# Moving one filler tile between the two scans of a Mamba-2 layer, and halving two fillers

## The chip, the core and the metric

The kernel runs on one core of a Trainium2 chip. The metric is device time in microseconds (us) of one execution; the median of three runs stands for a kernel. Five engines work side by side, each through its own instructions in order: PE (TensorE, matmuls; PEld is its weight load), DVE (VectorE), ACT (ScalarE), POOL (GpSimd) and SP (SyncE, which issues all DMAs here). They wait for each other on semaphores.

## The reference

One encoder layer with 1024 tokens of width 1024: a half feed-forward step, an input projection, then attention and a state-space part (SSD) side by side, an output projection `concat(a, s) @ W_out`, a second feed-forward step and a gated embedding. The change lies in the state-space part and in the half of the output projection that belongs to attention. What the state-space part computes, per direction, in 8 chunks of 128 tokens (8 heads of width 64, two groups, state of 128):

```python
seg = a_cum[..., :, None] - a_cum[..., None, :]
Lmat = jnp.exp(jnp.where(tril, seg, -jnp.inf))
cb = jnp.einsum('bclgn,bcsgn->bcgls', c_c, b_c)
y_diag = jnp.einsum('bcgls,bgrcls,bcsgrp->bclgrp', cb, Lmat, xd)
decay_states = jnp.exp(a_cum[..., -1:] - a_cum)
states = jnp.einsum('bcsgn,bgrcs,bcsgrp->bcgrpn', b_c, decay_states, xd)
# scan over chunks: h -> h * d + st, prev is h before the chunk
y_off = jnp.einsum('bclgn,bcgrpn,bgrcl->bclgrp', c_c, prev, jnp.exp(a_cum))
...
y = y_f + y_b + d_skip * xh
y = y * silu(z);  y = rms over each group of 256;  ssd_out = y * ssd_norm
mix = concat(att_out, ssd_out) @ w_out
```

The backward direction is the same scan over the flipped sequence.

## The kernel before

All PE instructions stand in the order in which the program is written. The other engines' instructions, and SP's DMAs, are put in an order by a scheduler that knows the dependencies; it may move them past each other.

The state-space part follows the attention and has two passes over the chunks.

**The right pass** (`ssd_right`) runs from chunk 7 down to chunk 0 in a software pipeline of ten turns `i = 0 .. 9`. Turn i does `front` of chunk 7-i, `mid`, `offdiag` and `next_state` of chunk 8-i, and `back` of chunk 9-i:

- `front` (PE L1348, then ACT L1350; PE L1354, then ACT L1356): the decay exponents of both directions in two PSUM tiles, their exponentials `Ef` and `Eb`, and the product `cb` of B and C. It also loads the chunk two further on.
- `mid` (DVE L1361, L1362, L1365): `y` is the skip term; `W = (Eb + Ef) * cb` for both directions at once.
- `offdiag` (PE L1270, then DVE L1272 and L1273): C times the state that came from the chunks before, scaled, added to `y`.
- `next_state` (ACT L1264 scales x into `xs`, PE L1281, ACT L1264 scales the old state by the chunk's decay, DVE L1287 adds; for a first state DVE copies, L1284).
- `back` (PE L1371, DVE L1372): W times x, added to `y`, and a DMA stores `y` to `yd` in DRAM (L1373). There are three `y` buffers, so `mid` of a chunk waits for the store of the chunk three before it.

**The left pass** (`ssd_left`) runs from chunk 0 up to 7 with the forward direction's `offdiag` and `next_state`, loads `y` back from `yd`, adds, multiplies by the gate z (L1439), normalises (L1443 to L1449) and transposes `y` on PE for the output projection (`turn`, L1417, three chunks behind).

**Fillers** stand between the steps of both passes: PE work that depends on nothing near. A filler is the attention half of the output projection for one row tile of 128 tokens: it loads the residual row from `y0` in DRAM into an accumulator, does 24 matmuls (L122) in two column halves of 12, and adds each half's PSUM tile into the accumulator on DVE (`out_proj`, L1464; L1466 in the changed kernel). Row tiles 0 to 2 run in the right pass (`spilled`), and their accumulators `accr` (two buffers) go out to `y1` in DRAM; row tiles 3 to 7 run in the left pass (`resident`) and their accumulators `acc` stay in SBUF, in memory that the right pass's accumulators use before. All matmul results of both passes, but the exponents, share four PSUM buffers `sm`.

Before the change row tiles 0 and 1 stand at the end of turns 0 and 1, row tile 2 stands in turn 8 ahead of that turn's `offdiag` (chunk 0), and the left pass begins with the whole of row tile 3, then its first `next_state`, then `offdiag` of chunk 1.

Of the kernel before, what the change touches and what calls it, by code (L numbers as in the profile page):

```python
# [9 lines left out]
F32 = mybir.dt.float32  # L10
# [3 lines left out]
ALU = mybir.AluOpType  # L14
# [4 lines left out]
P = 128  # L19
S = 1024  # L20
D = 1024
NT = S // P
# [14 lines left out]
class Layer:  # L37
# [1288 lines left out]
    def ssd_right(self, c, loaded, fillers):  # L1326

        nc, tc = self.nc, self.tc
        V = nc.vector
# [29 lines left out]
        def mid(ch, xb, bc, E, cb):  # L1359
            y = two.tile([P, 512], F32, name="y", bufs=3)  # L1360
            V.tensor_tensor(out=self.heads(y), in0=self.heads(xb[:, :512]), in1=self.per_head(dsk), op=ALU.mult)  # L1361
            V.tensor_tensor(out=E[1], in0=E[1], in1=E[0], op=ALU.add)  # L1362
            W = E[1]
            for g in range(2):
                V.tensor_tensor(out=W[:, 4 * g:4 * g + 4], in0=W[:, 4 * g:4 * g + 4], in1=cb[:, g].unsqueeze(1).broadcast_to([P, 4, P]), op=ALU.mult)  # L1365
            return W, y

        def back(ch, xb, bc, W, y):
# [7 lines left out]
        F, B = {}, {}  # L1376
        for i in range(NT + 2):
            ch = NT - 1 - i
            if ch >= 0:
                F[ch] = front(ch)  # L1380
            if 0 <= ch + 1 < NT:
                c1 = ch + 1
                xb, bc, E, cb = F.pop(c1)
                B[c1] = (c1, xb, bc) + mid(c1, xb, bc, E, cb)
                if c1 == 0:
                    fillers.pop(i)()
                if st is not None:
                    self.offdiag(two, st, 1, c1, bc, B[c1][4])
                if c1 > 0:
                    st = self.next_state(two, st, 1, c1, xb)  # L1390
            if ch + 2 < NT:
                back(*B.pop(ch + 2))
            if i in fillers:
                fillers[i]()

    def ssd_left(self, c, loaded, late, mixT, fillers):

        nc, tc = self.nc, self.tc
        V = nc.vector
# [26 lines left out]
        for ch in range(NT):  # L1426
            xb, bc = loaded[ch]
            zs, y = rest.pop(ch)
            if st is not None:
                self.offdiag(two, st, 0, ch, bc, y)  # L1430
            if ch == 0:
                fillers.pop(0)()
            if ch < NT - 1:
                st = self.next_state(two, st, 0, ch, xb)
            if len(waiting) > 2:
                turn(*waiting.pop(0))
            if 0 < ch < NT - 1:
                load(ch + 1)
            V.tensor_tensor(out=y, in0=y, in1=zs, op=ALU.mult)  # L1439
            ss = self.small.tile([P, 2], F32, name="yss")  # L1440
            for g in range(2):
                sq = late.tile([P, 256], F32, name="ysq")
                nc.scalar.activation(out=sq, in_=y[:, g * 256:(g + 1) * 256], func=AF.Square, accum_out=ss[:, g:g + 1])  # L1443
            V.tensor_scalar(out=ss, in0=ss, scalar1=1.0 / 256, scalar2=RMS_EPS, op0=ALU.mult, op1=ALU.add)
            r = self.small.tile([P, 2], F32, name="yr")
            self.rsqrt(r, ss, 2)
            for g in range(2):
                o = slice(g * 256, (g + 1) * 256)
                V.scalar_tensor_tensor(out=y[:, o], in0=y[:, o], scalar=r[:, g:g + 1], in1=snorm[:, o], op0=ALU.mult, op1=ALU.mult)  # L1449
            waiting.append((ch, y))  # L1450
            if ch:
                fillers.pop(0)()
# [78 lines left out]
    def run(self):  # L1531
        nc, tc, I = self.nc, self.tc, self.I
# [6 lines left out]
        y0 = self.dram.tile([NT, P, D], F32, name="y0")  # L1539
# [29 lines left out]
        with ExitStack() as c:  # L1569
# [12 lines left out]
            mixT = [[self.unit(h, 0)] for h in range(2)]  # L1582
# [6 lines left out]
        wm = [[], []]  # L1589
# [13 lines left out]
                blocks = blocks0  # L1603
            wm[half].extend(zip(blocks[:4], blocks[4:]))

        def attention_half(t, a):
            nc.sync.dma_start(out=a, in_=y0[t])
            self.out_proj(t, 0, wm[0], mixT, a)

        sctx = ExitStack()  # L1610
        late = sctx.enter_context(tc.tile_pool(name="slate", bufs=2))
        self.ld = sctx.enter_context(tc.tile_pool(name="sload", bufs=4))
        loaded = {}
        with ExitStack() as c:
            def spilled(t):
                a = self.accr.tile([P, D], F32, name="accr")
                attention_half(t, a)
                nc.sync.dma_start(out=y1[t], in_=a)

            weights(0)  # L1620
            for h in range(2):
                mixT[h].append(self.unit(h, 1))
            self.ssd_right(c, loaded, {i: lambda t=t: spilled(t) for t, i in enumerate((0, 1, 8))})
        rctx.close()
        actx = ExitStack()
        ap = actx.enter_context(tc.tile_pool(name="acc1", bufs=8, side="right"))
# [3 lines left out]
            nc.sync.dma_start(out=dst, in_=I[name])  # L1630
        acc = {}

        def resident(t):
            acc[t] = ap.tile([P, D], F32, name="acc1")
            attention_half(t, acc[t])
            if t == NT - 1:
                weights(1)

# [23 lines left out]
        def mixed(t):  # L1662
            r = Row(t)
            for step in (lambda: r.half(0), lambda: r.half(1), r.root, r.factors, r.shift):
                step()
# [13 lines left out]
                nc.scalar.activation(out=to[k // 4][:, k % 4], in_=ps[k // 4][:, k % 4], func=AF.Identity, scale=gT[:, k:k + 1], bias=bT[:, k:k + 1])  # L1679

        with ExitStack() as c:
            fillers = [lambda t=t: resident(t) for t in range(3, NT)] + [lambda t=t: mixed(t) for t in range(3)]
            self.ssd_left(c, loaded, late, mixT, fillers + [lambda: mixed(3), lambda: (flip(0), mixed(4))])
        sctx.close()
        dctx.close()
# [289 lines left out]
```

## Time and profile before

| | |
|---|---|
| time, median of 3 runs | 1952.08 us (1951.97 to 1953.29) |
| the profiled execution's own time | 1952.0 us |
| its span, first to last instruction | 1950.2 us |
| PE busy | 1927.4 us, 99% of the span |
| DVE busy | 1526.2 us, 78% |
| ACT busy | 880.9 us, 45% |
| the right and the left pass on PE | from 1064.6 to about 1189 us of the span |

The profile's times count from the first instruction. A row of the timeline has start, length, engine, source line, operation, tiles and how many equal instructions it merges; in brackets stands how long the engine sat idle before it and what released it. A matmul's length reaches to the modelled arrival of its result, while the next one starts earlier, so how long a group keeps PE is read from the start of one group to the start of the next. An fp32 matmul shows as two.

### The profile page before, as it was taken

How to read it: one execution, taken by the hardware profiler on the slowest of the kernel's cores; microseconds unless marked ns; L12 is line 12 of the kernel's file. 1: busy time of each engine (PE TensorE's matmuls, PEld its weight loads, DVE VectorE, ACT ScalarE, POOL GpSimd, SP SyncE). 2: the span in 40 equal slices, each digit the busy share in tenths (PEclk: the TensorE clock that was granted, in tenths of full speed). 3: DMA queues.
4: the chain of work that ended last, by engine and by line, in shares of the span. 5: the costliest groups of instructions: out<-in, count | busy, mean ns of one | idle time of the engine just before them, and what ended most of it. 6: DMA issues, size and time to landing. Idle time of an engine off the chain costs nothing.

```text
span 1950.2 us, 25647 instructions
## 1 busy us (share of the span) xinstructions
PE 1927.4 (99%) x9132; PEld 1607.7 (82%) x9132; DVE 1526.2 (78%) x2364; ACT 880.9 (45%) x1509; POOL 416.0 (21%) x310
## 2 busy tenths in 40 slices
PE   8999999999999999999999999999999999999998
PEld 7888888888888889888888788888888888888886
DVE  7977777867678658758998878997686777877698
ACT  6433333325444224537887775733333333443311
POOL 0144545430001032001221001013544440001011
PEclk9999999999999999999999999999999999999999
DMA  8434554549866111231002383244545439986122
GB/s 301 138 125 154 191 179 151 194 164 373 294 221 208 61 38 59 82 120 61 6 1 88 132 290 114 92 161 163 189 155 185 163 129 354 334 262 225 33 76 98
DMA packets 147713, 310.34 MB, mean 159 GB/s; under 512 B 18128, under 2 KB 30800, under 8 KB 147584
## 3 DMA queue, kind: packets, MB, share of 16 engines
q1 hardware_dynamic: 147584, 308.69, 45.2%
q8 instruction: 72, 1.18, 0.3%
q14 instruction: 57, 0.47, 0.1%
HBM read 217.21 MB, written 91.42 MB: 158 GB/s over the span
## 4 chain that ended last, share of the span: by engine, by line
PE 95%; DVE 3%; ACT 1%; issue 0%; DMA 0%; POOL 0%; DVEq 0%; SPq 0%; ACTq 0%
PE sm L122 59%; PE big L516 12%; PE sm L516 9%; PE big L122 3%; PE big L1159 3%; PE sm L1181 2%; PE sm L1196 1%; PE sm L1197 1%; PE sm L1270 1%; PE sm L1371 1%; DVE nm L1166 1%; DVE conv L977 1%; PE sm L1281 0%; PE big L1677 0%; PE big L224 0%
## 5 line engine op out<-in xcount | busy, mean ns | idle before, releaser
L122 PE MATMUL sm<-xh,blk 128*128 128x512 f32 x1424 | 439.9, 389 | 0.0
L122 PEld LDWEIGHTS sm<-xh,blk 128*128 128x128 f32 x1424 | 267.3, 188 | 55.4
L122 PE MATMUL sm<-xl,blk 128*128 128x512 f32 x736 | 283.8, 389 | 0.0
L122 PE MATMUL sm<-blk,xl 128*128 128x512 f32 (+2 forms) x784 | 238.1, 371 | 0.2 <-ACT xn_t L1010 0.2
L122 PE MATMUL sm<-blk,xh 128*128 128x512 f32 (+2 forms) x584 | 202.7, 378 | 0.4 <-DVE accr L1464 0.4
L108 ACT CAST blk<-raw 128x512 fp32r<-128x512 f32 (+1 forms) x168 | 101.1, 610 | 214.6 <-PE sm L122 132.0
L87 DVE TENSOR_TENSOR blk<-s,blk 128x512 fp32r<-128x512 f32 x176 | 150.1, 857 | 38.3 <-ACT blk L108 36.5
L87 DVE TENSOR_TENSOR blk<-raw,blk 128x512 fp32r<-128x512 f32 (+1 forms) x168 | 144.9, 866 | 38.4 <-ACT blk L108 37.6
L108 ACT CAST blk<-s 128x512 fp32r<-128x512 f32 x172 | 105.8, 622 | 145.1 <-PE sm L122 114.7
L122 PEld LDWEIGHTS sm<-blk,xl 128*128 128x128 f32 x784 | 142.8, 188 | 24.2 <-ACT xn_t L1010 0.5
L122 PEld LDWEIGHTS sm<-xl,blk 128*128 128x128 f32 x736 | 138.1, 188 | 28.7
L178 POOL TENSOR_TENSOR ln_k<-ln_k,mhalf 128x1 f32<-128x1 f32 x32 | 36.6, 1149 | 583.3 <-DVE ln_k L177 578.3
L516 PE MATMUL big<-xh 128*128 128x512 f32 x576 | 138.8, 390 | 0.0
L267 POOL TENSOR_TENSOR s<-raw 128x512 f32<-128x512 f32 x34 | 55.1, 1620 | 384.4 <-DVE blk L87 378.2
L87 DVE TENSOR_TENSOR xh<-blk,xh 128x1024 fp32r<-128x1024 f32 x78 | 96.4, 1236 | 46.2 <-ACT xh L462 37.1
L462 ACT CAST xl<-blk 128x1024 fp32r<-128x1024 f32 x76 | 80.2, 1055 | 115.1 <-PE sm L516 41.4
L462 ACT CAST xh<-blk 128x1024 fp32r<-128x1024 f32 x78 | 82.3, 1055 | 106.0 <-PE big L516 49.2
L122 PEld LDWEIGHTS sm<-blk,xh 128*128 128x128 f32 x584 | 109.8, 188 | 19.9 <-DVE accr L1464 0.8
L516 PEld LDWEIGHTS big<-xh 128*128 128x128 f32 x576 | 107.8, 188 | 22.2
L87 DVE TENSOR_TENSOR xl<-blk,xl 128x1024 fp32r<-128x1024 f32 x76 | 92.6, 1219 | 41.9 <-ACT xl L462 37.2
L516 PE MATMUL big<-xl 128*128 128x512 f32 x480 | 115.7, 390 | 0.0
L122 PE MATMUL sm<-xET2h,blk 128*128 128x512 f32 x352 | 108.4, 389 | 0.0
(343 smaller groups left out, 4014.0 us busy)
## 6 DMA issues: line engine op xcount, KB each, us to landing
raw<-in_wi_dram SPq DMA_DIRECT2D x81, 512.0 KB
blk<-hS SPq DMA_DIRECT2D x154, 256.0 KB
hS<-h SPq DMA_DIRECT2D x88, 256.0 KB
wr<-in_wo_dram SPq DMA_DIRECT2D x44, 512.0 KB
blk<-wT SPq DMA_DIRECT2D x88, 256.0 KB
hS<-sg SPq DMA_DIRECT2D x66, 256.0 KB
wT<-wr SPq DMA_DIRECT2D x66, 256.0 KB
blk<-in_wo_dram SPq DMA_DIRECT2D x66, 256.0 KB
```

The lines of the kernel that those rows point to most:

```text
L87: (eng or self.nc.vector).tensor_tensor(out=out, in0=full, in1=hi.bitcast(F32), op=ALU.subtract)
L108: self.nc.scalar.copy(out=b[:, 0, :n], in_=src)
L122: self.nc.tensor.matmul(ps, lhsT=a, rhs=b, start=(i == 0), stop=(i == n - 1))
L178: nc.gpsimd.tensor_tensor(out=r, in0=v, in1=self.mhalf[:, :1], op=ALU.pow)
L267: lambda: G.tensor_tensor(out=s1, in0=a21, in1=a22, op=ALU.add),
L462: A.copy(out=b[:, :, 0], in_=r)
L516: nc.tensor.matmul(ps[q], lhsT=b[:, 0, x, cut], rhs=b[:, 1, y], start=j == i == 0, stop=j == NP - 1 and i == 2)
L977: nc.vector.scalar_tensor_tensor(out=a[:, o], in0=ps[:, o.start + d - c:o.stop + d - c], scalar=cw[:, j, tap:tap + 1], in1=a[:, o], op0=AL ...
L1159: nc.tensor.matmul(ps[:, n * 512:(n + 1) * 512], lhsT=Q[:, h, q0:q0 + P], rhs=K[:, h // 4, j, n * 512:(n + 1) * 512], start=j == 0, stop=j ...
L1166: nc.vector.tensor_reduce(out=nm, in_=ps, axis=AX.X, op=ALU.max, negate=True)
L1181: nc.tensor.transpose(out=pt[:, k], in_=pr[:, kk * P:(kk + 1) * P], identity=self.ident)
L1196: nc.tensor.matmul(po, lhsT=vw, rhs=pth[k // 4][:, k % 4], start=k == 0, stop=False)
```

## The change

Four edits:

- Row tile 2 leaves turn 8. Its first column half now stands at the end of turn 4 (behind `back` of chunk 5) and its second at the end of turn 5 (behind `back` of chunk 4). The accumulator's load goes with the first half, its store to `y1` with the second.
- In turn 8, where row tile 2 stood, `back` of chunk 1 now stands ahead of `offdiag` of chunk 0.
- In the left pass row tile 3 runs in halves too, and the first `next_state` stands between them.
- In `mid` the product with `cb` is one DVE instruction of 1024 elements per partition instead of two of 512 (one for each group).

```diff
             W = E[1]
-            for g in range(2):
-                V.tensor_tensor(out=W[:, 4 * g:4 * g + 4], in0=W[:, 4 * g:4 * g + 4], in1=cb[:, g].unsqueeze(1).broadcast_to([P, 4, P]), op=ALU.mult)
+            Wg = W.rearrange("p (g h) l -> p g h l", g=2)
+            V.tensor_tensor(out=Wg, in0=Wg, in1=cb.unsqueeze(2).broadcast_to([P, 2, 4, P]), op=ALU.mult)
...
                 if c1 == 0:
-                    fillers.pop(i)()
+                    back(*B.pop(1))
                 if st is not None:
                     self.offdiag(two, st, 1, c1, bc, B[c1][4])
...
-            if ch + 2 < NT:
+            if ch + 2 in B:
                 back(*B.pop(ch + 2))
             if i in fillers:
                 fillers[i]()
...
             if ch < NT - 1:
                 st = self.next_state(two, st, 0, ch, xb)
+            if ch == 0:
+                fillers.pop(0)()
...
-            self.ssd_right(c, loaded, {i: lambda t=t: spilled(t) for t, i in enumerate((0, 1, 8))})
+            self.ssd_right(c, loaded, {0: lambda: spilled(0), 1: lambda: spilled(1), 4: lambda: spilled(2, (0,)), 5: lambda: spilled(2, (1,))})
...
-            fillers = [lambda t=t: resident(t) for t in range(3, NT)] + [lambda t=t: mixed(t) for t in range(3)]
+            fillers = [lambda n=n: resident(3, (n,)) for n in range(2)] + [lambda t=t: resident(t) for t in range(4, NT)] + [lambda t=t: mixed(t) for t in range(3)]
```

(`spilled`, `resident` and `attention_half` take the halves `ns` to do: the load comes with half 0, the store of a spilled row with half 1.) The work is the same in amount on every engine but for the eight DVE instructions that are merged. Outside the two passes each engine's order is as before.

The end of the right pass on PE, as a difference. L122 is a filler, L1371 `back`, L1270 `offdiag`; the first two rows are turn 7:

```order
 L1270 MATMUL sm<-state,bc 128x256 x2
 L1281 MATMUL sm<-xs,xb 128x256 x2
+L1371 MATMUL sm<-xb,Eb 128x64 x16
+L1270 MATMUL sm<-state,bc 128x256 x2
 L1371 MATMUL sm<-xb,Eb 128x64 x8
 L122 MATMUL sm<-blk,xh_7565 128x512
```

Behind turn 7's two steps PE now does `back` of chunks 2 and 1, `offdiag` and `back` of chunk 0, with no filler between; the L122 row that follows is the left pass's first half.

ACT at the same place, as a difference; the `Ef` and `Eb` that are added are chunk 0's, and `state` is the old state's scaling in chunk 1's `next_state`:

```order
 L1264 ACTIVATE state<-state,cd 128x64 x8
 L1350 ACTIVATE Ef<-big 128x2x8x64
 L1350 ACTIVATE Eb<-big 128x2x8x64
 L1356 COPY cb<-sm 128x256
-L1264 ACTIVATE state<-state,cd 128x64 x8
+L1350 ACTIVATE Ef<-big 128x2x8x64
+L1264 ACTIVATE state<-state,cd 128x64 x6
+L1350 ACTIVATE Eb<-big 128x2x8x64
+L1264 ACTIVATE state<-state,cd 128x64 x2
+L1356 COPY cb<-sm 128x256
 L1264 ACTIVATE xs<-xb,sdt 128x64 x24
```

Six of the eight scalings now stand between the two exponentials of chunk 0.

DVE from chunk 0's `W` to the left pass's first state, before. `Eb_10095` is chunk 0's W, `state_10125` the state that `offdiag` of chunk 0 reads, `y_10146` chunk 0's y, `acc1_10237` row tile 3's accumulator, `state_10279` the left pass's first state:

```order
L1365 TENSOR_TENSOR Eb_10095<-Eb_10095,cb_10100 128x512 x2
L1361 TENSOR_TENSOR y_10146<-xb_9959,dsk_7563 128x512
...
L1372 TENSOR_TENSOR y_10146<-y_10146,sm_10199 128x512
L1464 SCALAR_TENSOR_TENSOR acc1_10237<-sm_10239,acc1_10237 128x512
L1464 SCALAR_TENSOR_TENSOR acc1_10237<-sm_10253,acc1_10237 128x512
L1284 COPY state_10279<-sm_10276 128x512
```

And now, where `Eb_10120`, `state_10149`, `y_10170`, `acc1_10229` and `state_10257` are the same five (`y_10067` and `y_10127` are chunks 2 and 1):

```order
L1362 TENSOR_TENSOR Eb_10120<-Eb_10120,Ef_10115 128x1024
L1287 TENSOR_TENSOR state_10149<-state_10149,sm_10146 128x512
L1372 TENSOR_TENSOR y_10067<-y_10067,sm_10159 128x512
L1365 TENSOR_TENSOR Eb_10120<-Eb_10120,cb_10125 128x1024
L1372 TENSOR_TENSOR y_10127<-y_10127,sm_10174 128x512
L1272 TENSOR_TENSOR toff_10188<-sm_10185,eF_7024 128x512
L1466 SCALAR_TENSOR_TENSOR acc1_10229<-sm_10231,acc1_10229 128x512
L1361 TENSOR_TENSOR y_10170<-xb_9971,dsk_7563 128x512
L1284 COPY state_10257<-sm_10254 128x512
```

Chunk 0's skip term `y_10170` moved behind row tile 3's first half, directly ahead of the left pass's first state.

SP's queue, now, from row tile 2's store on (`acc<-y` from `y0` for row tiles 3 to 7, from `y1` for 0 to 2; `yd` takes the right pass's y):

```order
L1625 DMA y_9615<-accr 128x1024
L1610 DMA acc_10229<-y_86 128x1024
...
L1652 DMA acc_10892<-y_9615 128x1024
L1373 DMA yd<-y 128x512 x2
L1249 DMA bc<-bcT 128x4x128
L1373 DMA yd<-y 128x512
L1247 DMA xb<-xbn 128x768
L1373 DMA yd<-y 128x512
L1249 DMA bc<-bcT 128x4x128
L1409 DMA y_10221<-yd 128x512
```

The eight accumulator loads (512 KB each) follow row tile 2's store as before, but the stores of the last four chunks, which before stood ahead of them or between them, now stand behind all eight. The left pass's loads of `y` (L1409) stay behind both.

More of the change, by code (lines that the diff above doesn't have):

```diff
@@ L1604, in weights, with attention_half @@
             wm[half].extend(zip(blocks[:4], blocks[4:]))
-        def attention_half(t, a):
-            nc.sync.dma_start(out=a, in_=y0[t])
-            self.out_proj(t, 0, wm[0], mixT, a)
+        def attention_half(t, a, ns=(0, 1)):
+            if 0 in ns:
+                nc.sync.dma_start(out=a, in_=y0[t])
+            self.out_proj(t, 0, wm[0], mixT, a, ns)
         sctx = ExitStack()
@@ L1614, in run, with spilled @@
         with ExitStack() as c:
[L1615 to L1618, printed above, removed]
+            rows = {}
+            def spilled(t, ns=(0, 1)):
+                if 0 in ns:
+                    rows[t] = self.accr.tile([P, D], F32, name="accr")
+                attention_half(t, rows[t], ns)
+                if 1 in ns:
+                    nc.sync.dma_start(out=y1[t], in_=rows.pop(t))
             weights(0)
@@ L1631, in run, with resident @@
         acc = {}
-        def resident(t):
-            acc[t] = ap.tile([P, D], F32, name="acc1")
-            attention_half(t, acc[t])
+        def resident(t, ns=(0, 1)):
+            if 0 in ns:
+                acc[t] = ap.tile([P, D], F32, name="acc1")
+            attention_half(t, acc[t], ns)
             if t == NT - 1:
```

## The prediction

> **What bounds the kernel now.** I read the page's head first, then the busy time by stage for the two passes, then PE's timeline in the stages where PE is not full, and last the timelines of ACT, DVE and SP around those places.
>
> ```profile
> span 1950.2 us, 25647 instructions
> PE 1927.4 (99%) x9132; PEld 1607.7 (82%) x9132; DVE 1526.2 (78%) x2364; ACT 880.9 (45%) x1509; POOL 416.0 (21%) x310
> ```
>
> PE is the bound: all that can be won without taking matmuls away is its idle time. By stage (stretch, its length, then busy time of PE, PEld, DVE, ACT and POOL, granted clock, DMA share, GB/s):
>
> ```profile
> 1094.10:1113.20 19.10, 14.95 (x98) 12.65 (x97) 17.95 (x27) 17.00 (x54) 0.00 (x0) 1.00 0.25 84
> 1128.70:1132.20 3.50, 2.72 (x14) 2.04 (x13) 1.84 (x3) 2.37 (x10) 0.00 (x0) 1.00 1.00 393
> ```
>
> Here PE idles 4.15 and 0.78 us while DVE and ACT are almost full: turns 5 to 7 of the right pass, and the start of the left one. PE's own rows:
>
> ```profile
> 1090.19 0.61 PE L1354 MATMUL sm<-bc 128*128 128x128 f32 x4
> 1090.63 1.03 PE L1270 MATMUL sm<-state,bc 128*128 128x256 f32 x4
> 1091.50 1.03 PE L1281 MATMUL sm<-xs,xb 128*128 128x256 f32 x4
> 1092.36 1.89 PE L1371 MATMUL sm<-xb,Eb 128*128 128x64 f32 x16
> 1094.10 1.03 PE L1348 MATMUL big<-RT,LT 128*128 128x512 bf16 x4
> 1094.96 0.61 PE L1354 MATMUL sm<-bc 128*128 128x128 f32 x4
> 1097.23 1.10 PE L1270 MATMUL sm<-state,bc 128*128 128x256 f32 x4 [1.67 <-ACT xs L1264]
> 1098.17 1.03 PE L1281 MATMUL sm<-xs,xb 128*128 128x256 f32 x4
> ...
> 1101.63 0.61 PE L1354 MATMUL sm<-bc 128*128 128x128 f32 x4
> 1103.85 1.13 PE L1270 MATMUL sm<-state,bc 128*128 128x256 f32 x4 [1.61 <-DVE state L1287]
> ...
> 1107.41 1.03 PE L1348 MATMUL big<-RT,LT 128*128 128x512 bf16 x4
> 1108.28 0.61 PE L1354 MATMUL sm<-bc 128*128 128x128 f32 x4
> 1109.75 1.13 PE L1270 MATMUL sm<-state,bc 128*128 128x256 f32 x4 [0.86 <-DVE state L1287]
> ...
> 1113.28 0.48 PE L122 MATMUL sm<-blk,xh 128*128 128x512 f32 x1
> ...
> 1118.85 1.02 PE L1270 MATMUL sm<-state,bc 128*128 128x256 f32 x4
> ...
> 1123.20 0.47 PE L122 MATMUL sm<-blk,xh 128*128 128x512 f32 x1
> ...
> 1128.77 1.02 PE L1281 MATMUL sm<-xs,xb 128*128 128x256 f32 x4
> 1130.58 1.13 PE L1270 MATMUL sm<-state,bc 128*128 128x256 f32 x4 [0.78 <-DVE state L1284]
> 1131.55 1.03 PE L1281 MATMUL sm<-xs,xb 128*128 128x256 f32 x4
> ```
>
> From start to start, undisturbed: front 0.86 + 0.44 (L1348, L1354), `offdiag` 0.87, `next_state` 0.86, `back` 1.74 (1092.36 to 1094.10), so 4.77 a chunk; a filler 5.57 (1113.28 to 1118.85), a half 2.78. What a stall costs is the step's excess over these, and the slower restart behind it:
>
> - turn 5: 1097.23 - 1094.96 - 0.44 = 1.83, restart 1098.17 - 1097.23 - 0.87 = 0.07: 1.90
> - turn 6: 1103.85 - 1101.63 - 0.44 = 1.78, restart taken as 0.08: 1.86
> - turn 7: 1109.75 - 1108.28 - 0.44 = 1.03, and 0.08: 1.11
> - left pass: 1130.58 - 1128.77 - 0.86 = 0.95, restart 1131.55 - 1130.58 - 0.87 = 0.10: 1.05
>
> Together 5.92 us. Behind the stage, and ahead of the left pass's second chunk, PE runs full. Order and work elsewhere are unchanged, so what is won here should arrive at the end.
>
> **The change part by part.** The rows of the other engines that it rests on:
>
> ```profile
> 1096.41 0.68 DVE L1287 TENSOR_TENSOR state<-state,sm 128x512 f32<-128x512 f32 x1
> ...
> 1107.81 1.28 DVE L1365 TENSOR_TENSOR Eb<-Eb,cb 128x512 f32<-128x512 f32 x2
> ...
> 1110.21 1.22 DVE L1362 TENSOR_TENSOR Eb<-Eb,Ef 128x1024 f32<-128x1024 f32 x1
> ...
> 1129.83 0.69 DVE L1284 COPY state<-sm 128x512 f32<-128x512 f32 x1 [0.17 <-PE sm L1281]
> ...
> 1138.64 0.69 DVE L1439 TENSOR_TENSOR y<-y,zs 128x512 f32<-128x512 f32 x1 [2.60 <-DMA y<-yd]
> ```
>
> ```profile
> 1108.04 1.02 ACT L1350 ACTIVATE Ef<-big 128x1024 f32<-128x1024 f32 x1 [1.04 <-PE big L1348]
> 1108.96 1.02 ACT L1350 ACTIVATE Eb<-big 128x1024 f32<-128x1024 f32 x1
> ...
> 1110.12 2.02 ACT L1264 ACTIVATE state<-state,cd 128x64 f32<-128x64 f32 x8
> 1123.48 3.93 ACT L1264 ACTIVATE xs<-xb,sdt 128x64 f32<-128x64 f32 x16 [11.33 <-PE sm L1371]
> ```
>
> *Halves in turns 4 and 5.* In turn 5 the state is ready at 1097.09 (1096.41 + 0.68), 1.7 us after PE could take it (1095.40). The first half puts PE at 1094.10 + 2.78 + 1.30 = 1098.18: the wait goes, with 1.05 us to spare. The second half stands 3.47 us later (0.87 + 0.86 + 1.74) at 1101.65, turn 6 begins at 1104.43, its `offdiag` at 1105.73; before, its state was ready just ahead of 1103.85, and its links now start no later, so that wait goes too. Turn 7's `offdiag` comes at 1105.73 + 4.77 = 1110.50. Its state needs turn 6's sum, in DVE order behind L1272, L1362 and L1273: PE delivers to L1272 at 1105.73 + 1.03 = 1106.76, then steps of 0.60, 1.14 and 0.60 (start to start: the pair of L1365 is 1.28, one of 512 is 0.68; a 1024 is 1.22, which ends 0.08 into the next), then 0.68 and 0.14 to PE (1097.09 to 1097.23): 1109.9. It just fits, with 0.6. So the three stalls, 4.87 us, go. The half's own PSUM tiles and its DVE additions are the ones that were in turn 8.
>
> *Turn 8 without its filler.* This uncovers work that 5.57 us of matmuls hid. PE arrives at `back` of chunk 1 at 1110.50 + 0.87 + 0.86 + 1.74 = 1113.97, at `offdiag` of chunk 0 at 1115.71, at `back` of chunk 0 at 1116.58. Chunk 0's W comes by this chain, from its front's start at 1110.50 - 1.30 = 1109.20: to Ef 0.63 (1107.41 to 1108.04), Ef 0.92 (start to start), six scalings of 0.24 each ((2.02 - 0.10) / 8) 1.44, Eb 1.02, then DVE L1362 1.14, L1287 0.60, L1372 0.60, L1365 at its merged size 1.22, and 0.14 to PE: 7.71, so 1116.91, which is 0.33 late. With the restart and small gaps between engines I take 0.50. The bounds: nothing, if ACT lets the scalings overlap better, and 1.9, the largest stall of these rows, if the chain runs as badly as turn 5's. The state for `offdiag` of chunk 0 comes out at 1109.20 + 0.63 + 0.92 + 1.44 + 1.02 + 1.14 + 0.68 + 0.14 = 1115.2, 0.5 ahead of need.
>
> *Left pass in halves.* xs starts 0.28 after the last `back` (1123.48 against 1123.20) and eight of its activations take 2.02, so it is ready 2.4 us behind it with the gap to PE; half 0 covers 2.78. Then half 1 stands between `next_state` and `offdiag`: 3.64 us where the copied state needs 1.75 (1130.52 - 1128.77). In DVE's queue the copy now waits behind the first half's addition (2.78 + 0.2 after `back`) and chunk 0's skip term, 0.60 each, so it can end at about 4.9 us behind `back`, while PE needs it at 2.78 + 0.86 + 2.78 = 6.4. The 1.05 goes.
>
> *The merged product* saves 1.28 - 1.22 = 0.06 us of DVE eight times, hidden everywhere but in the chain above, where it is in the 1.22. [...]
>
> *SP.* The accumulators' loads come early, which takes away DVE's wait for them at the left pass's start; the price is in the rivals. `back` of chunk 1 ahead of `offdiag` costs nothing: W of chunk 1 is an ACT and DVE turn older.
>
> Sum: 4.87 + 1.05 - 0.50 = 5.42 us. The profiled execution took 1952.0, its span 1950.2, so 1944.8 of span; the median, 1952.08, is the profiled time within 0.1. Forecast 1952.08 - 5.42 = 1946.7 us.
>
> **The rivals.**
>
> A. *ACT stays the bound at the tail.* The slacks in turns 7 and 8 are about half a microsecond each, and ACT was 17.00 of 19.10 busy. If two of the links slip, the uncovered stall is 1.9 instead of 0.50: gain 4.0, 1948.1. Against it: ACT gains twice 2.78 on PE in turns 4 and 5.
>
> B. *The left pass's transposes wait for y.*
>
> ```profile
> 1119.77 0.32 SPq L1618 DMA_DIRECT2D y<-accr  x1
> ...
> 1122.77 2.18 SPq L1607 DMA_DIRECT2D acc<-y  x3
> 1125.05 0.38 SPq L1373 DMA_DIRECT2D yd<-y  x1
> ...
> 1126.80 1.93 SPq L1644 DMA_DIRECT2D acc<-y  x3
> 1131.63 1.75 SPq L1409 DMA_DIRECT2D y<-yd  x4
> ```
>
> ```profile
> 1144.17 0.88 DVE L1449 SCALAR_TENSOR_TENSOR y<-y,yr,snorm 128x256 f32<-128x256 f32 x2
> 1146.79 0.60 PE L1417 MATMUL sm<-ident,y 128*128 128x128 f32 x4
> ```
>
> Chunk 0's y is now finished behind row tile 3's first half, 6.2 us after the last `back`, instead of 0.9. PE ends that `back` at 1118.8 and reaches the transposes 22.5 us later (1146.79 - 1123.20 - 1.05) at 1141.3. The store goes at 1125.0; store to load took 6.58 (1125.05 to 1131.63) and load to use 7.0 amid the eight big loads, then 6.4 to the scaled y (1145.05 - 1138.64): 1145.0, 3.7 late at worst, 1950.4. But those loads now start some 14 us earlier and are over by then; without them both DMAs should take less than half, and y is early. A partial wait of 1.9 gives 1948.6.
>
> C. *The other side: the store of chunk 3's y holds DVE.* SP issues it behind row tile 2's store and eight loads. Chunk 0's skip term needs that buffer, and the left pass's first state stands behind it on DVE. Row tile 2's second half ends at 1104.43, its sum about 0.9 later; 3.0 us for its store (1119.77 to 1122.77) put the loads at 1108.4, their issue takes under 6 (1122.77 to 1128.73), so the store goes at 1114.4 and lands at 1121.0 by the 6.58 of B. DVE wants it at 1122.4, PE feels it from 1123.8 on. From 1129.2 on the whole gain is eaten; landing at 1133.2, 12 us later than this sum, it would give 1956.0.
>
> D. *It does little.* If DVE, 17.95 of 19.10 busy, sets the pass's length, the stalls move to turns 6 to 8 and only the left pass's 1.05 and the merges (0.5) are won: 1950.5. Against it: right behind the stage, from 1113.28 on, PE is full in a filler that DVE uses to catch up.
>
> **How the numbers follow.** The forecast's case, with the residue between 0 and 1.3, has 0.62; A 0.15, B 0.10, C 0.05 (and 0.01), D 0.07. No change that this measurement can tell is 0.2%, 3.9 us, so faster means under 1948.2. The forecast's case gives 0.62, A 0.12 and B 0.03 to faster: 0.77; the rest of A and B and all of D make 0.17 for the same, and C, with 0.01 for trouble that I have no name for, 0.06 for slower. The low end is all 5.92 won and 0.5 for the spread of the runs: 1945.7. The high end takes in A, and B to within 0.4 of its worst: 1950.0. It leaves out D and C and the tip of B, and some runs below the low end, together under 2 in 10.
>
> **What the new profile would show.** PE's idle time in the right pass drops to one stall of about half a microsecond ahead of the last `back`, L1371; no L1270 row has a bracket in turns 5 to 7 or at the left pass's start; the first transposes L1417 start near 1141.4; the span is near 1944.8. Wrong would be: an L1270 row still released by DVE L1287 (A, D), an L1417 that waits for DVE L1451 (B), a DVE row of L1361 that waits for `yd<-y` near 1122 (C), or a gain that is there at the transposes and gone at the end, which nothing here predicts.

## The result: 4.7 us faster, with the stalls gone where they were forecast and a new one behind them

| | before | changed |
|---|---|---|
| median | 1952.8 us (10 runs, 1951.97 to 1954.42) | 1947.9 us (10 runs, 1947.74 to 1948.79) |
| ratio of the runs | | 0.9976, 95% interval 0.9967 to 0.9984: 4.7 us, 3.1 to 6.4 |
| the profiled execution | 1952.0 us, span 1950.2 | 1948.74 us, span 1946.9 |
| first L1348 to first transposes L1417 | 82.16 us | 76.79 us |
| first L1348 to the last matmul (*the stretch*, below) | 876.31 us | 872.31 us |

The stretch, from PE's timeline, start to start, is what single profiles are compared by: the first L1348 lies anywhere between 1064.4 and 1065.8 us in these profiles, though the program ahead of it is the same in all of them, and that offset says nothing on the change (it is 0.64 between the two profiles above). Three single executions in the experiments' sets, two of the kernel before at 2152 us and one of the left halves with later loads at 3230, stand far outside the rest and are not read.

The head of the changed kernel's page, and its busy time in the two stretches that were shown of before (length, then PE, PEld, DVE, ACT, POOL, granted clock, DMA share, GB/s):

```profile
span 1946.9 us, 25645 instructions
...
PE 1927.9 (99%) x9132; PEld 1607.8 (83%) x9132; DVE 1528.0 (78%) x2356; ACT 881.1 (45%) x1509; POOL 416.9 (21%) x310
```

```profile
1094.10:1113.20 19.10, 19.10 (x114) 15.97 (x114) 17.65 (x24) 16.31 (x54) 0.00 (x0) 1.00 0.51 168
1128.70:1132.20 3.50, 3.50 (x17) 2.89 (x16) 0.58 (x1) 3.10 (x13) 0.00 (x0) 1.00 0.88 261
```

PE is busy throughout both, where it was idle for 4.15 and 0.78 us. Its timeline in turns 5 to 8 of the right pass, at the left pass's start and at the first transposes:

```profile
1098.95 1.03 PE L1270 MATMUL sm<-state,bc 128*128 128x256 f32 x4
...
1106.54 1.03 PE L1270 MATMUL sm<-state,bc 128*128 128x256 f32 x4
...
1111.31 1.03 PE L1270 MATMUL sm<-state,bc 128*128 128x256 f32 x4
...
1113.04 3.68 PE L1371 MATMUL sm<-xb,Eb 128*128 128x64 f32 x32
1116.55 1.08 PE L1270 MATMUL sm<-state,bc 128*128 128x256 f32 x4
1117.68 1.97 PE L1371 MATMUL sm<-xb,Eb 128*128 128x64 f32 x16
...
1125.93 1.02 PE L1270 MATMUL sm<-state,bc 128*128 128x256 f32 x4
...
1142.06 0.65 PE L1417 MATMUL sm<-ident,y 128*128 128x128 f32 x4
1143.86 0.50 PE L122 MATMUL sm<-blk,xh 128*128 128x512 f32 x1 [1.15 <-DVE acc L1466]
```

No L1270 has a bracket. What is left in the right pass is the step from the last L1270 to the last L1371, 1.13 us instead of 0.87. From the first L1348 to the transposes 82.16 - 76.79 = 5.37 us are won. Then a stall that before did not have: row tile 6's first half (L122) waits for a PSUM buffer that DVE frees late. It costs 1143.86 - 1142.06 - 0.36 = 1.44 us (0.36 is the step from L1417 to L122 without a wait), and 4.00 us arrive at the end.

Where that stall comes from is told by the chain of waits ahead of it (start, length, what):

```profile
1112.64 11.51 DMA yd<-y
...
1124.25 0.06 DVE y L1361
...
1126.89 2.04 DMA yd<-y
1128.95 0.32 SPq L1409
...
1131.21 3.65 DMA raw<-in_wm_dram
...
1136.72 0.63 ACT blk L108
...
1137.38 0.04 DVE blk L87
...
1141.42 0.79 DVE y L1451 x2
...
1143.20 0.61 DVE acc L1466
```

The store of chunk 3's y takes 11.51 us and holds chunk 0's skip term (L1361). Chunk 0's y is finished and stored only then; behind that store SP issues the left pass's loads of y (L1409), and behind these the loads of the second weight half (`raw`, L1602), which ACT and DVE split (L108, L87) for the output projection's other half. DVE, in order, reaches the first scalings of y (L1451) and the accumulation (L1466) late. DVE's own rows there:

```profile
1122.50 0.69 DVE L1466 SCALAR_TENSOR_TENSOR acc<-sm,acc 128x512 f32<-128x512 f32 x1 [3.73 <-PE sm L122]
1124.25 0.69 DVE L1361 TENSOR_TENSOR y<-xb,dsk 128x512 f32<-128x512 f32 x1 [1.05 <-DMA yd<-y]
...
1131.62 0.69 DVE L1441 TENSOR_TENSOR y<-y,zs 128x512 f32<-128x512 f32 x1 [2.97 <-DMA y<-yd]
...
1137.38 0.69 DVE L87 TENSOR_TENSOR blk<-raw,blk 128x512 fp32r<-128x512 f32 x1 [1.19 <-ACT blk L108]
...
1141.34 0.88 DVE L1451 SCALAR_TENSOR_TENSOR y<-y,yr,snorm 128x256 f32<-128x256 f32 x2
```

The first row is as telling as the second: for 3.73 us ahead of 1122.50 DVE stood idle, with chunk 0's skip term behind row tile 3's first addition in its order. Three things could thus be to blame: that order, the slow store, and the weight splits. The experiments separate them.

### The profile page after: what moved, and what is told of

The parts are those of the page before. It is cut to its first block, busy times and chain, and to the rows that moved or that the text cites. A ratio compares the mean times of both kernels' runs of the same rounds, so it can differ in the third digit from the quotient of the medians.

```text
span 1946.9 us, 25645 instructions
## 1 busy us (share of the span) xinstructions
PE 1927.9 (99%) x9132; PEld 1607.8 (83%) x9132; DVE 1528.0 (78%) x2356; ACT 881.1 (45%) x1509; POOL 416.9 (21%) x310
## 3 DMA queue, kind: packets, MB, share of 16 engines
q8 instruction: 72, 1.18, 0.2%
## 4 chain that ended last, share of the span: by engine, by line
PE 94%; DVE 3%; DMA 1%; ACT 1%; issue 1%; POOL 0%; SPq 0%; DVEq 0%; ACTq 0%
PE sm L122 59%; PE big L516 12%; PE sm L516 9%; PE big L122 3%; PE big L1159 3%; PE sm L1181 2%; PE sm L1196 1%; PE sm L1197 1%; DMA yd<-y 1%; DVE nm L1166 1%; DVE conv L977 1%; PE sm L1270 0%; PE big L224 0%; PE sm L224 0%; PE big L909 0%
## 5 line engine op out<-in xcount | busy, mean ns | idle before, releaser
L122 PE MATMUL sm<-xh,blk 128*128 128x512 f32 x1424 | 439.8, 389 | 0.0
L122 PEld LDWEIGHTS sm<-xh,blk 128*128 128x128 f32 x1424 | 267.3, 188 | 55.4
L122 PE MATMUL sm<-xl,blk 128*128 128x512 f32 x736 | 283.8, 389 | 0.0
L122 PE MATMUL sm<-blk,xl 128*128 128x512 f32 (+2 forms) x784 | 238.2, 371 | 0.2 <-ACT xn_t L1010 0.2
L122 PE MATMUL sm<-blk,xh 128*128 128x512 f32 (+2 forms) x584 | 203.3, 379 | 1.6 <-DVE acc L1466 1.1
L108 ACT CAST blk<-raw 128x512 fp32r<-128x512 f32 (+1 forms) x168 | 101.3, 611 | 215.0 <-PE sm L122 134.1
L87 DVE TENSOR_TENSOR blk<-s,blk 128x512 fp32r<-128x512 f32 x176 | 150.8, 861 | 35.2 <-ACT blk L108 33.2
L87 DVE TENSOR_TENSOR blk<-raw,blk 128x512 fp32r<-128x512 f32 (+1 forms) x168 | 146.5, 875 | 40.6 <-ACT blk L108 40.1
L108 ACT CAST blk<-s 128x512 fp32r<-128x512 f32 x172 | 105.7, 622 | 146.5 <-PE sm L122 118.3
L122 PEld LDWEIGHTS sm<-blk,xl 128*128 128x128 f32 x784 | 142.8, 188 | 24.2 <-ACT xn_t L1010 0.5
L122 PEld LDWEIGHTS sm<-xl,blk 128*128 128x128 f32 x736 | 138.2, 188 | 28.6
L87 DVE TENSOR_TENSOR xh<-blk,xh 128x1024 fp32r<-128x1024 f32 x78 | 95.4, 1223 | 48.4 <-ACT xh L462 42.3
L122 PEld LDWEIGHTS sm<-blk,xh 128*128 128x128 f32 x584 | 109.9, 188 | 21.3 <-DVE acc L1466 1.4
L87 DVE TENSOR_TENSOR xl<-blk,xl 128x1024 fp32r<-128x1024 f32 x76 | 92.7, 1220 | 41.3 <-ACT xl L462 36.7
L122 PE MATMUL sm<-xET2h,blk 128*128 128x512 f32 x352 | 108.4, 389 | 0.0
```

The lines of the kernel that those rows point to most:

```text
L87: (eng or self.nc.vector).tensor_tensor(out=out, in0=full, in1=hi.bitcast(F32), op=ALU.subtract)
L108: self.nc.scalar.copy(out=b[:, 0, :n], in_=src)
L122: self.nc.tensor.matmul(ps, lhsT=a, rhs=b, start=(i == 0), stop=(i == n - 1))
```

## The experiments

They ran in four sets, each on one chip together with the kernel before, to which the ratios refer; its median lay between 1952.5 and 1953.3 us in these sets. The stretch is that of one profiled execution; two profiles of the changed kernel lie 0.84 us apart (872.31 and 871.47), so smaller differences of the stretch alone say little.

| kernel | median us | ratio, 95% interval | stretch us |
|---|---|---|---|
| right pass's part alone | 1948.71 | 0.9980 (0.9971 to 0.9989) | 872.18 |
| left pass's halves alone | 1957.61 | 1.0025 (1.0016 to 1.0035) | 881.01 |
| four `y` buffers | 1946.58 | 0.9971 (0.9960 to 0.9982) | 870.76 |
| weight splits later | 1946.78 | 0.9972 (0.9960 to 0.9983) | 870.72 |
| two products | 1948.55 | 0.9977 (0.9967 to 0.9986) | 871.35 |
| old order in turn 8 | 1948.78 | 0.9979 (0.9970 to 0.9988) | 872.82 |
| four buffers and later splits | 1946.35 | 0.9967 (0.9954 to 0.9979) | 870.06 |
| later accumulator loads | 1947.45 | 0.9972 (0.9961 to 0.9983) | 871.25 |
| row tile 2 whole in turn 4 | 1946.64 | 0.9969 (0.9958 to 0.9980) | 870.45 |
| left halves, later accumulator loads | 1953.02 | 1.0001 (0.9991 to 1.0010) | 876.47 |
| row tile 2 whole, four buffers | 1946.32 | 0.9966 (0.9953 to 0.9979) | 870.09 |
| the changed kernel again | 1947.99 | 0.9976 (0.9967 to 0.9985) | 871.47 |

**The right pass's part alone.** The changed kernel with the left pass as before:

```diff
-            if ch == 0:
-                fillers.pop(0)()
...
-            fillers = [lambda n=n: resident(3, (n,)) for n in range(2)] + [lambda t=t: resident(t) for t in range(4, NT)] + ...
+            fillers = [lambda t=t: resident(t) for t in range(3, NT)] + ...
```

> The right pass as changed, the left pass as before: row tile 3 whole ahead of the first next_state. My theory: the three stalls of turns 5 to 7 go, a rest of about 0.4 us at the last back stays, and the left pass's stall of 0.78 us at L1270 (1.05 with its restart) is there again. That leaves 4.4 us of gain at the first transposes, and since PE then comes 1 us later to row tile 6, the new stall of 1.15 us at L122 behind the transposes shrinks to 0.5 or less: 4.0 to 4.4 us faster than before. Rival, the two parts do not add up (the left halves alone bring the late stall): the whole of the late stall goes, and this kernel is as fast as the full change or faster.

The stretch is 4.13 us shorter than before, as expected (3.8 by the medians); 0.3 of it lies in the first fillers, which have nothing to do with the left pass. PE keeps the old stall at the left pass's start and has less of the late one (line numbers of L1466 are L1464 here):

```profile
1126.42 1.13 PE L1270 MATMUL sm<-state,bc 128*128 128x256 f32 x4 [0.78 <-DVE state L1284]
...
1143.69 0.50 PE L122 MATMUL sm<-blk,xh 128*128 128x512 f32 x1 [0.46 <-DVE acc L1464]
```

So the left pass's halves take 0.78 away and the late stall grows by 0.69 (by 0.30 in the changed kernel's second profile, below). What they add on top is 0.8 us by the medians, with intervals that overlap.

**The left pass's halves alone.** The kernel before with the left pass in halves and the merged product; row tile 2 whole, in turn 8:

```diff
                 if c1 == 0:
-                    back(*B.pop(1))
+                    fillers.pop(i)()
...
-            self.ssd_right(c, loaded, {0: lambda: spilled(0), 1: lambda: spilled(1), 4: lambda: spilled(2, (0,)), 5: lambda: spilled(2, (1,))})
+            self.ssd_right(c, loaded, {i: lambda t=t: spilled(t) for t, i in enumerate((0, 1, 8))})
```

> The left pass as changed (row tile 3 in halves, the first state between them), the right pass as before with row tile 2 in turn 8. My theory: the stalls of turns 5 to 7 stay (1.67, 1.61, 0.86 us), only the left pass's 1.05 us go: 0.8 to 1.1 us faster than before. Rival, the halves also bring the late stall at row tile 6 by themselves, because DVE does the accumulation and the skip term ahead of the first state: then 0 or up to 0.5 us slower.

A miss for both theories: 4.70 us longer. PE's timeline at turn 7, and from the first transposes on:

```profile
1110.58 1.10 PE L1270 MATMUL sm<-state,bc 128*128 128x256 f32 x4 [1.62 <-DVE state L1287]
...
1145.74 1.03 PE L1281 MATMUL sm<-xs,xb 128*128 128x256 f32 x4
1149.96 0.83 PE L1417 MATMUL sm<-ident,y 128*128 128x128 f32 x4 [3.19 <-DVE y L1451]
1150.55 0.47 PE L122 MATMUL sm<-blk,xh 128*128 128x512 f32 x1
...
1151.78 0.63 PE L122 MATMUL sm<-blk,xl 128*128 128x512 f32 x1
...
1155.89 0.39 PE L122 MATMUL sm<-blk,xl 128*128 128x512 f32 x1
...
1157.73 1.02 PE L1270 MATMUL sm<-state,bc 128*128 128x256 f32 x4
```

```profile
1147.00:1162.00 15.00, 12.04 (x50) 9.78 (x51) 13.04 (x37) 8.27 (x34) 1.39 (x2) 0.89 0.59 192
```

The left pass's stall is gone (-1.05), turn 7's is larger (1.62 instead of 0.86: +0.76), and the transposes wait for y: 1149.96 - 1145.74 - 0.87 = 3.35. Behind that wait matmuls of one shape take 0.63 us and later 0.39, the granted clock over the stage is 0.89 where it is 1.00 in every other stretch shown, and the filler takes 1157.73 - 1150.55 = 7.18 us against 5.59 (1143.06 to 1148.65 in the changed kernel's second profile): +1.6. With 0.23 for the slower transposes these make 4.9, close to the 4.70 measured. The chain of waits ahead of the transposes runs through the accumulators' loads and the chunk loads behind them:

```profile
1124.01 6.62 DMA acc<-y
...
1130.69 9.19 DMA xb<-xbn
...
1139.96 2.02 ACT xs L1264 x8
```

That is rival B of the prediction, in a kernel in which the eight loads were not moved early: from the store of chunk 0's y to its load 6.84 us, from load to use 8.0, from use to the end of L1451 9.7 (the prediction had 6.58, 7.0 and 6.4). The last of the three is the one that grew: ACT had waited 3.62 us for a chunk load behind the same eight and squared y for the normalisation only at 1143.81, 2.5 us after y was multiplied by the gate. The two parts of the change do not add: -4.13 and +4.70 alone, -4.00 (and -4.84 in the second profile) together.

**Four `y` buffers**, the changed kernel otherwise, so that chunk 0's skip term needs no store to have landed:

```diff
-            y = two.tile([P, 512], F32, name="y", bufs=3)
+            y = two.tile([P, 512], F32, name="y", bufs=4)
```

> The full change with four y buffers in the right pass in place of three, so that chunk 0's skip term (L1361) no longer waits for the store of chunk 3's y. If that hold (1.05 us on DVE at 1124) makes the late stall at row tile 6, by way of the store and the load of chunk 0's y, the load that DVE waits for comes 1 us earlier, and the stall of 1.15 us shrinks to 0.4 or less: 0.8 to 1.3 us faster than the changed kernel, 5.3 us faster than before. If the late stall comes from the order of DVE's work or from the loads of the output weights, it stays at 1.0 to 1.2 us and the time is that of the changed kernel, 4.0 to 4.9 faster than before.

**The second half's weight splits later**, behind row tile 5's work on ACT and DVE:

```diff
-                        blocks += [self.split(h) for h in halves]
+                        with self.behind(mybir.EngineType.Activation), self.behind(mybir.EngineType.DVE):
+                            blocks += [self.split(h) for h in halves]
...
-            if t == NT - 1:
+            if t == 5:
```

> The full change, but the splitting of the output projection's second-half weights (ACT L108 and DVE L87, which come in among the normalisations of the left pass's first chunks and held DVE 1.19 us at 1136 while ACT waited for their DMA) is queued behind the work traced up to row tile 5. If that hold makes the late stall, it is gone: L122 behind the first transposes starts without a wait, and the kernel is 1.2 to 1.5 us faster than the changed one, 5.4 us faster than before. If it is the late y alone, DVE still has 2.97 us of waiting at L1441 and the stall keeps half or more of its size. If later work pays for the moved splits (the first mixed row tile needs them), a new stall stands at L122 behind row tile 7.

Both are shorter than the changed kernel's first profile by 1.6 us (870.76 and 870.72), than its second by 0.7, and by the medians by 1.3 and 1.1. With four buffers the late stall is 0.44, near what was expected, and a stall that before has too (0.41 there, 0.49 in the changed kernel, in the first fillers) is gone. The buffers are the cause of that: the step from turn 1's L1281 to its first L122 is 0.67 to 0.68 us in the three kernels with four buffers and 1.11 to 1.54 in the eleven profiles with three. With later splits the late stall is gone and that older one stays, at 0.38:

```profile
1122.44 0.69 DVE L1361 TENSOR_TENSOR y<-xb,dsk 128x512 f32<-128x512 f32 x1
...
1129.83 0.69 DVE L1441 TENSOR_TENSOR y<-y,zs 128x512 f32<-128x512 f32 x1 [1.98 <-DMA y<-yd]
```

```profile
1141.28 0.60 PE L1417 MATMUL sm<-ident,y 128*128 128x128 f32 x4
1141.64 0.48 PE L122 MATMUL sm<-blk,xh 128*128 128x512 f32 x1
```

Chunk 0's skip term starts here 57.8 us after the first L1348, still behind row tile 3's first addition, and its y is used at 65.2: as late as in the changed kernel's second profile (57.6 and 65.1), which loses 1.00 us. So a late y alone does not make the stall; the weight splits that DVE does in between are part of it. **Both together:**

> The changed kernel with four y buffers and with the second weight splits behind row tile 5's work. Theory (both take away the same late stall): no more than the better of the two alone, 870.5 to 870.8 us from the first L1348 to the last matmul, the stall at the last back (0.26) being what is left. Rival (they remove different waits that add): 869.8 to 870.2.

The stretch is 870.06, within the rival's range: the theory was wrong, since neither stall is left, and each part removes one that the other leaves (the first fillers' and the rest of the late one), 0.7 us.

**The later accumulator loads.** Six of the eight stand behind the left pass's first loads of y in SP's queue:

```diff
+        def fetch(t):
+            acc[t] = ap.tile([P, D], F32, name="acc1")
+            nc.sync.dma_start(out=acc[t], in_=(y1 if t < 3 else y0)[t])
...
+            if t == 3 and 0 in ns:
+                fetch(3)
+                fetch(4)
+            elif t > 3:
+                with self.behind(mybir.EngineType.SP):
+                    for u in {4: (5, 6), 5: (7, 0), 6: (1,), 7: (2,)}[t]:
+                        fetch(u)
...
```

> The changed kernel, but six of the eight accumulator loads stand later in SP's queue, behind the left pass's first loads of y. Theory (the store of chunk 3's y landed 11.5 us after its issue because it stood behind eight loads of 512 KB): its store lands within 6 us, DVE's L1361 no longer waits for it, and the late stall of 1.45 us goes: 870.7 to 871.3 us from the first L1348 to the last matmul. Rival (the store is slow for another reason, or the moved loads hold something else up): L1361 waits as before, or an L1466 waits for its load, and the time is 872 or more.

SP's queue, then DVE's and PE's timeline:

```profile
1108.76 0.80 SPq L1642 DMA_DIRECT2D acc<-y  x2
1112.40 5.00 SPq L1373 DMA_DIRECT2D yd<-y  x2
```

```profile
1115.18 0.69 DVE L1361 TENSOR_TENSOR y<-xb,dsk 128x512 f32<-128x512 f32 x1
```

```profile
1118.30 1.97 PE L1371 MATMUL sm<-xb,Eb 128*128 128x64 f32 x16 [0.59 <-PE sm L1270]
```

The store of chunk 3's y, issued at 1112.40, has landed by 1115.18, at most 2.8 us later: two loads ahead of it instead of eight, and 11.51 us become 2.8. The late stall is gone. The theory held, at the upper end of its range, because the skip term now stands ahead of chunk 0's state and W on DVE: the chain to the last `back` is 0.6 longer, and the step from the last L1270 to the last L1371 is 1.69 instead of 1.13. Chunk 0's y is used at 61.0 us after the first L1348 instead of 66.4, so the splits that are still there do no harm.

**The left halves alone, with the later loads:**

> The left pass's halves alone on the kernel before, and six of the eight accumulator loads later in SP's queue, behind the left pass's first loads of y. The left halves alone took 881.01 us from the first L1348 to the last matmul, the kernel before 876.31. Theory (they lost because chunk 0's y was read back amid the eight loads, PE then waited 3.2 us at the transposes, and its granted clock fell to 0.89 over the next stage): without the loads in the way y is there in time, the wait at L1417 is under 1 us, the clock 1.00, and the time 875.2 to 876.8. Rival (the halves cost PE that much by their own order, or the copied state and DVE are the limit): 879 or more, with the wait at L1417 still for DVE's L1451.

```profile
1098.27 1.10 PE L1270 MATMUL sm<-state,bc 128*128 128x256 f32 x4 [1.88 <-DVE state L1287]
...
1111.43 1.10 PE L1270 MATMUL sm<-state,bc 128*128 128x256 f32 x4 [1.57 <-DVE state L1287]
...
1147.44 0.60 PE L1417 MATMUL sm<-ident,y 128*128 128x128 f32 x4
```

```profile
1147.00:1162.00 15.00, 15.00 (x72) 12.61 (x71) 11.78 (x29) 11.50 (x44) 1.39 (x2) 1.00 0.85 299
```

No wait at the transposes, the clock at 1.00, the stretch 876.47: 4.54 of the 4.70 were the loads. That it is no faster than before lies in turn 7, where L1270 waits 1.57 instead of 0.86, and in turn 5 (1.88 instead of 1.67); 0.92 of the 1.05 go there.

**Row tile 2 whole, at the end of turn 4:**

```diff
-            self.ssd_right(c, loaded, {0: lambda: spilled(0), 1: lambda: spilled(1), 4: lambda: spilled(2, (0,)), 5: lambda: spilled(2, (1,))})
+            self.ssd_right(c, loaded, {0: lambda: spilled(0), 1: lambda: spilled(1), 4: lambda: spilled(2)})
```

> The changed kernel with row tile 2 whole at the end of turn 4 instead of in halves behind turns 4 and 5. Theory (what counts is that ACT and DVE get 5.57 us ahead of turn 5, not where the halves stand): turns 5 and 6 have no stall, and turn 7, which loses 2.78 us of cover gained only once, none or under 0.4; the stall at the last back stays 0.2 to 0.6; 872.0 to 872.9 us from the first L1348 to the last matmul. Rival (ACT and DVE need longer a turn than PE's 4.77, so that the lead is spent by turn 7): stalls of 0.5 to 1 us at L1270 in turns 6 and 7, 873 to 874.

Better than both theories: 870.45, no stall in turns 5 to 7 and no late one. Its DVE rows:

```profile
1119.07 0.69 DVE L1361 TENSOR_TENSOR y<-xb,dsk 128x512 f32<-128x512 f32 x1
...
1131.64 0.88 DVE L1451 SCALAR_TENSOR_TENSOR y<-y,yr,snorm 128x256 f32<-128x256 f32 x2
```

The 5.57 us of lead last through turn 7, wherever the halves stand, and row tile 2's store, with the eight loads and the stores of y behind it, goes earlier. Chunk 0's skip term starts 54.6 us after the first L1348 instead of 59.0, its scaling at 67.2 instead of 76.1. **With four `y` buffers as well:**

> Row tile 2 whole at the end of turn 4, and four y buffers. Row tile 2 whole has 870.44 us from the first L1348 to the last matmul, with one stall left of those that this case is about, 0.45 us in the first fillers, behind DVE's skip terms that wait for a y buffer. Theory (the fourth buffer takes that one away and nothing else is left): 869.9 to 870.1 us, some 0.4 less than with three buffers. Rival (with four buffers the scheduler sets DVE's order anew, and the chain to the last back gets longer, as it did with the late loads, where L1371 waited 0.59): 870.4 to 871.0.

870.09 us, as the theory had it, though 0.21 us of waiting for the state is left at the last L1270, and 1946.32 us median, about as long as with both remedies on the halves (1946.35). These two are the shortest. The stall that went was not a wait for a `y` buffer, as the expectation calls it: DVE's first addition (L1466) waited 0.79 us for its accumulator's load, which SP issues 5.0 us behind the first L1348 with three buffers and 4.1 us ahead of it with four. Why the load can go earlier with four was not asked.

**Two products instead of the merged one**, the old two lines:

> The changed kernel with the product with cb in two DVE instructions of 512 again. Theory (the merge saves 0.06 us where nobody waits and 0.06 in the chain to the last back): from the first L1348 to the last matmul the time is within 0.15 us of the changed kernel's 872.31, its stall at the last back 0.26 to 0.4. [...]

871.35 us, with a late stall of 0.53. This lies 0.96 below the changed kernel's first profile and 0.12 below its second; by the medians it is 0.65 and 0.56 above. The theory missed, and so did its stall: the step at the last `back` is 0.92, shorter than the changed kernel's 1.13. By the medians the two products cost something, by the traces they do not: there DVE uses chunk 0's y no later than in the changed kernel (65.2 us after the first L1348 against 66.4 and 65.1), and the intervals overlap. What the merge is worth stays open; it is less than a microsecond.

**The old order in turn 8** (`back` of chunk 1 behind `offdiag` of chunk 0):

```diff
                 if c1 == 0:
-                    back(*B.pop(1))
+                    pass
```

> The changed kernel with back of chunk 1 behind offdiag of chunk 0 again, where it stood before. Theory (this swap is what gives chunk 0's state its 1.74 us): PE waits about 1.2 us (0.9 to 1.7) at the last L1270 for DVE's state, in place of 0.26 ahead of the last L1371; from the first L1348 to the transposes about 0.9 us more than the changed kernel's 76.79. But the late stall of 1.45 us behind the transposes is a wait for DVE, which does not depend on PE's arrival: it shrinks by about as much, so to the last matmul 872.3 to 872.6. Rival (a stall is a stall, each adds to the end): 873.2 to 873.4.

```profile
1116.28 1.13 PE L1270 MATMUL sm<-state,bc 128*128 128x256 f32 x4 [0.97 <-DVE state L1287]
...
1144.89 0.50 PE L122 MATMUL sm<-blk,xh 128*128 128x512 f32 x1 [0.94 <-DVE acc L1466]
```

The stall at the last L1270 is there as expected, the late one is hardly smaller (1.18 us lost). By the medians the swap is worth 0.8 to 0.9 us, but the stretch, 872.82, lies between the two theories; whether part of the early stall is absorbed by the late one stays open. In this kernel chunk 0's skip term stands ahead of row tile 3's addition on DVE, and waits 3.54 us for the store of chunk 3's y: it starts at 57.6 us after the first L1348, as late as behind the addition.

**The changed kernel again:**

> The changed kernel once more, unchanged, for the spread of its late stall from one execution to the next. Theory (the stall is a sum of waits for transfers, whose landings vary): it is anywhere from 0 to 1.2 us in a profiled execution, with 871.0 to 872.5 us from the first L1348 to the last matmul, and the gain up to the transposes is again 5.2 to 5.7. Rival (the stall is fixed by the order of the instructions): 1.0 to 1.3 us again, 872.2 to 872.5.

A late stall of 0.76 (1143.06 - 1141.70 - 0.36 = 1.00 lost), and 82.16 - 76.38 = 5.78 us won up to the transposes, just above what was expected; 0.38 of the 0.41 more than in the first profile lies in the first fillers (the step of 1.52 there is 1.14 here). The stall and its chain of waits:

```profile
1143.06 0.50 PE L122 MATMUL sm<-blk,xh 128*128 128x512 f32 x1 [0.76 <-DVE acc L1466]
```

```profile
1119.29 2.83 PE sm L122 x12
...
1122.91 0.06 DVE y L1361
...
1129.83 5.24 DMA raw<-in_wm_dram
```

Here the slow store had landed in time: the chain behind the stall comes from PE, with row tile 3's first half, and L1361 follows that half's addition at once.

Taken together, the late stall needs two things. One is a late y of chunk 0, and either the skip term's place in DVE's order (this profile) or the slow store (the old order in turn 8) is enough for that. The other is the weight splits among the normalisations. Where y is used early (61.0 us after the first L1348 with later loads, 62.1 with row tile 2 whole) or the splits come later, the stall is gone; with y at 63.3 (four buffers) 0.68 us of it is left, at 65.1 to 66.4 it is 0.7 to 1.4.

## Why the prediction was right, and where it was not

- **The three stalls of turns 5 to 7 (4.87) and the left pass's (1.05)** went as forecast; PE is busy for 19.10 of 19.10 us. The gain up to the transposes was forecast at 5.42 and measured at 5.37 and 5.78. The first L1417 was forecast near 1141.4; it came at 1142.06, which is the forecast and the offset of 0.64 at the start.
- **The residue at the last `back`**, 0.50 in the sum, measured 1.13 - 0.87 = 0.26. The chain named for it is the right one: with a skip term of 0.60 put into it (later loads) it is 1.69 - 0.87 = 0.82.
- **"`back` ahead of `offdiag` costs nothing"**: it wins 0.8 to 0.9 us. In the old order PE waits 0.97 at the last L1270, where now 0.26 is lost ahead of the last L1371.
- **"What is won here should arrive at the end"** is the step that failed. It left out DVE's work behind the stage, which did not come forward as far as PE: the transposes came 5.37 us earlier, but the end of the scaling of chunk 0's y only 3.5 (76.95 instead of 80.42 us after the first L1348), and the splits of the second weight half now fell between the normalisations. 1.44 us in one profile and 1.00 in the other came back as a stall at row tile 6's first half. Of the prediction's own signs of being wrong two were seen: a row of L1361 that waits for `yd<-y`, and a gain that is there at the transposes and partly gone at the end, "which nothing here predicts".
- **Rival B was dismissed with "y is early".** It came just in time: by the prediction's own terms, with both DMAs at half, the scaled y comes at 1125.0 + 3.3 + 3.5 + 6.4 = 1138.2. Measured were a store at 1126.89, 2.06 from store to load, 2.67 from load to use and 10.6 from use to the end of L1451, 1142.22 in all. The DMAs shrank as argued; the mis-sized term is the 6.4. The weight splits, which did not stand there in the kernel before, explain only part of that: with the splits later the same term is 9.4 (1129.83 to 1139.23), so about 3 us of the growth come from elsewhere; from where was not tested. The transposes started at 1142.06 without a wait, and the work behind y on DVE was late instead.
- **Rival C's place** was right, its price was not. The store was issued at 1112.64, 1.8 earlier than its sum said, and took 11.51 instead of 6.58. It held L1361 for 1.05 us, but PE's L1270 at the left pass's start had room for that; the cost came 18 us later, and only in part from there, since the second profile, without that hold, still loses 1.00 of the 1.44.
- **A and D** are not seen: no L1270 waits for L1287 in these turns.
- **Halving.** The argument for two halves in turns 4 and 5 was sound, but not needed: the whole tile in turn 4 gives the same cover and frees SP's queue earlier.
- **The time.** Forecast were 1946.7 us and 5.42 of gain, from 1952.08; ten runs put the kernel before at 1952.8, so 0.7 of the 1.2 us between 1946.7 and 1947.9 lies in that base. The other 0.5 is gain: 4.9 by the medians instead of 5.42, and 4.00 and 4.84 by the two profiles. That the late stall took back about a microsecond, and not more, was worked out nowhere ahead: the left pass's halves alone cost 4.70 us by the same kind of wait. So the nearness of the time is in part luck. The median is under the 1948.2 that the prediction set for a change that can be told, but the interval of the ratio, 0.9967 to 0.9984, reaches across it. In five kernels whose late stall is 0.44 us or nothing (later splits, row tile 2 whole, and the three with four buffers) the medians are 1946.3 to 1946.8 us, 5.7 to 7.0 below the kernel before in their sets; with the later loads, 1947.45, PE waits at the last `back` instead. The three with four buffers win the first fillers' 0.7 as well, which the forecast did not count.

What stays open is why the late stall differs between executions of one kernel (1.15 and 0.76 by the brackets); the chains show transfers of different length (11.51 us, `raw` 3.65 and 5.24), not why they differ.

## What to carry to other kernels

When a stall of the bounding engine is removed, list what the other engines must have ready in the microseconds behind it, with the slack of each in the new schedule; work that was in time only because PE came late became the next stall here, of 1.44 and 1.00 us in two profiles. Follow moved work through the transfer queue as well: here a row tile that ended 14 us earlier moved eight loads of 512 KB, and where such loads stood decided whether the left pass's halves alone cost 4.70 us or, with six of the eight later, 0.16. Parts of a change that share a queue are tried alone and together, since their effects need not add (here -4.13 and +4.70 us alone, -4.00 together).

## What the runs showed of the hardware

- In the left halves alone a wait of 3.19 us on PE was followed by matmuls at 0.63 instead of 0.39 us (0.42 instead of 0.23 from start to start), for some 3.5 us, and cost 1.6 us beyond itself (granted clock 0.89 over the stage); waits of 1.67 us in the kernel before and of 1.88 in the left halves with later loads left the granted clock at 1.00 (1094.1 to 1113.2 in both).
- In the changed kernel a store of 256 KB took 11.51 us from issue to landing behind eight loads of 512 KB in SP's queue, while the 16 DMA engines' busy share was 1.00 (1112.6 to 1124.2, 370 GB/s); with the later loads, behind two, the same store took at most 2.8 us.
